# P1's stores on ScalarE's queue, two kept blocks in u's buffer, four operands no longer kept

## The chip, the core and the metric

The kernel runs on one core of a Trainium2 chip. The metric is the time of one execution on the device in microseconds; the time of a kernel is the median of several runs. A core has TensorE (matmuls into PSUM), VectorE, ScalarE, GpSimd and SyncE. In the profile they are PE (its weight loads apart, as PEld), DVE, ACT, POOL and SP. DMAs are issued by SyncE, ScalarE and GpSimd, each in the order of its own instructions.

## The reference, cut to what matters

```python
def reference(x, router_logits, expert_weights):
    # x (16, 512, 512), router_logits (16, 512, 8), expert_weights (8, 512, 2048), float32
    probs = softmax(router_logits, axis=-1)
    for e in range(8):
        output += probs[:, :, e:e+1] * np.matmul(x, expert_weights[e])
    return output          # (16, 512, 2048) float32
```

The sum over experts is one matrix product: the left side has 8192 rows (tokens) and 8 x 512 columns, x times the probability of expert e side by side; the right side is the eight weight matrices on top of each other, 4096 x 2048.

## The kernel before, in words

**Two levels of fast multiplication.** The large product is cut in two by two: token blocks of 256 rows go in pairs a = 2q and b = 2q + 1 (q = 0 to 15), the experts in two groups of four, the output columns in two halves of 1024. Instead of eight products of such parts the kernel does seven, called P1 to P7, with sums of left parts, of right parts and of results around them. Each of them is again done in seven steps (1, 5, 6, 2, 7, 3, 4 in that order, `STEPS`, line 389) of eight matmuls of 128 x 512, and in some stages four of the steps are done with a third level (`Third`, line 674). TensorE accumulates in PSUM; the other engines make the operands and carry the results on.

**Stages.** A stage holds two products (14 steps, "slots" of about 1.73 us), rarely one. In order: P1 of q = 2 to 15 is stages 0 to 6 (of q = 0, 1 it is done at the very start in another way); P2 is 7 to 14; P5 of q = 0, 1 is stage 15 (`k5`); P6 of q = 0 alone is stage 16; P6 of q with P5 of q + 1 is 17 to 30; P6 of 15 with P7 of 14 is 31 (`k7`); P4 and P7 are 32 to 46; 47 (`k3`) has the last P4 and P3 of q = 0; 48 has P3 of q = 14 and 15; 49 to 54 have P3 of 1 to 12 in pairs; 55 has P3 of 13. Stages 0 to 6, 8 to 12 and 49 to 54 have the third level.

**Order of work.** All engines keep the order in which the program writes their instructions. `at(stage, slot, ...)` (line 751) hangs work on a slot. VectorE's operands are tasks in one queue: `later(cost, make)` (line 415) appends one with a cost in us; `slack()` (line 420) runs at each slot, moves a counted clock on by 1.73 and writes down tasks until VectorE's counted clock has caught up; `evacuated()` counts 0.61 for a sum of a result. `need` (line 410) writes down what is needed at once. Loads of x and p blocks for a stage begin two stages before (`start_loads`, line 846), in nine buffers of `xpool`; P1's x blocks 16 to 30 are cast by GpSimd into the one buffer called u (`x_room`, line 435) and transposed by SyncE's DMA (line 463).

**What the change touches.**
- P1's results of q go to DRAM (`kept`) by `sink` in `product` (line 804): four blocks (0,0), (0,1), (1,0), (1,1) of 128 x 512, all stored from GpSimd's queue by `pool`. Step 2 gives (0,0) and step 4 gives (1,0), both copied from PSUM by ScalarE (line 627); step 7 gives (1,1) and step 3 (0,1), by VectorE (line 630).
- `Base.fetch` (line 738) loads such a block back from SyncE's queue into one of 13 buffers h. `fetch_at` (line 951) hangs the fetches of P2 on slots of the stage before it (lines 960 to 965), those of P6 on lines 993 to 997. P6 first takes P5's block off it (`joined`, line 989). The block is then the tile in which the result is summed and from which it is stored.
- `KEEP` (line 762): for these q the left operand of P6 is stored from SyncE's queue (line 1289, `kept_left`) and in P3 it is loaded back from ScalarE's queue (line 1290, `Operand`, line 563), so that P3's left operand is one product of x and p, less the loaded one. For other q the loaded part is made anew (`second` in `Left.makes`, line 507): x and p of the second block are loaded and multiplied into u, and then taken off.
- The odd block of the weights, (0, 1): `cast_odd` (line 1076) casts its matrices 12, 11, 22 and 21 in two halves each at the slots of line 1116; `odd_t` (line 1081) makes three differences and sums of them, each one VectorE instruction of 128 x 4096; `odd_t4` (line 1097), at stage 15, slot 4, takes the last off matrix 21.

Of the kernel before, what the change touches and what calls it, by code (L numbers as in the profile page):

```python
# [31 lines left out]
def kernel(  # L32
# [17 lines left out]
    C = H // P  # L50
    HE = E // 2
    NB = 512
# [12 lines left out]
    zpool = ctx.enter_context(tc.tile_pool(name="zpool", bufs=8))  # L65
# [8 lines left out]
    def h_tile(shape, dtype):  # L74
        return hpool.tile(shape, dtype, name="h", tag="h")

    def half():
        return h_tile([P, NB], f32)

    lg0 = [cpool.tile([P, 4, E], f32, name=f"lg0_{t}") for t in range(2)]  # L80
    for q, begin in enumerate((nc.scalar, nc.sync)):
        rows = ds(2 * q * HQ, HQ)
        begin.dma_start(out=lg0[0][:, ds(2 * q, 2), :],
                        in_=router_logits.flatten_outer_dims()[rows].rearrange("(p j) e -> p j e", p=P))
# [15 lines left out]
    def note(i):  # L100
        last[i.ins.engine] = i.ins
        if ordered[0]:
            tc.keep_in_program_order(i)

    def dve(i):
        last[i.ins.engine] = i.ins
        tc.keep_in_program_order(i)
# [3 lines left out]
    def tt(o, a, b, op):  # L111
        dve(nc.vector.tensor_tensor(out=o, in0=a, in1=b, op=op))  # L112
# [9 lines left out]
    def sp(o, i):  # L122
        note(nc.sync.dma_start(out=o, in_=i))

    def pool(o, i, **how):
        note(nc.gpsimd.dma_start(out=o, in_=i, **how))  # L126

    def bank():
        return psum.tile([P, NB], f32, name="ps", tag="ps")
# [29 lines left out]
    def kept_w(what, kn):  # L159
        if (what, kn) not in stored:  # L160
            stored[what, kn] = dram.tile([C, P, 2, NB] if what in TWOS else [P, K8, NB], f16, name="wd")
        kept_t = stored[what, kn]
        return kept_t.rearrange("a p b n -> p a b n") if what in TWOS else kept_t
# [47 lines left out]
    def cast_x(j):  # L211
        pool(xs0[:, ds(j, 2), :], x_f[ds(j * HQ, HQ), :].rearrange("(j p) h -> p j h", p=P))
# [350 lines left out]
    class Operand:  # L563
# [86 lines left out]
    class Split:  # L650
# [74 lines left out]
    def out_rows(q, odd, cols, tn):  # L725
        t, n = tn
        return out_f[ds((2 * q + odd) * HQ + t * HP, HP), ds(cols * NH + n * NB, NB)]

    def to_out(q, odd, cols, **how):
        return lambda tn, o: pool(out_rows(q, odd, cols, tn), o, **how)  # L730

    class Base:
# [2 lines left out]
        def __init__(self, source):  # L735
            self.source, self.t = source, {}

        def fetch(self, tn):
            self.t[tn] = half()
            sp(self.t[tn], self.source(tn))  # L740

        def __call__(self, tn):
# [8 lines left out]
    def at(stage, slot, make):  # L751
        hooks.setdefault((stage, slot), []).append(make)

    def add(*products):
        stages.append(products)
        return len(stages) - 1
# [2 lines left out]
    right = {r: Right() for r in (2, 5, 6, 7, 4, 3)}  # L759
    right[1] = Right(w, {p: Task(2.2, sums[p]) for p in (6, 7, 4)})  # L760
    lefts, xs, ps_, bases = {}, {}, {}, {}
    KEEP = range(1, 14)

    def xblock(h):
        if h not in xs:
            xs[h] = XBlock(h)
        return xs[h]

    def left_of(r, q, fresh=True):
# [15 lines left out]
        if r == 6:  # L785
            pt = PBlock(a, P1)
            return Left(xblock(a), pt, of=lefts[5, q]), [xblock(a), pt]
        if r == 3 and q in KEEP:
            pt = PBlock(a, P2)
# [7 lines left out]
    def kept_rows(q):  # L797
        return lambda tn: kept[q][tn[1], ds(tn[0] * HP, HP), :]

    def product(r, q, **how):  # L800
        left, loads = left_of(r, q)
        lefts[r, q] = left
        p = None
        if r == 1:
            def sink(tn, o):
                pool(kept_rows(q)(tn), o)
            p = Product(right[1], left, sink)
        elif r == 2:
            if q >= 14:
                base = products[1, q].o.__getitem__  # L810
            else:
                base = bases[2, q] = Base(kept_rows(q))
            p = Product(right[2], left, to_out(q, 0, 0), base)
        elif r == 5:
            bases[6, q] = m1 = Base(kept_rows(q))
            m1.task = {}

            p = Product(right[5], left, to_out(q, 1, 0))
        elif r == 6:
            m1 = bases[6, q]  # L820

            def base(tn):
                need(m1.task[tn])
                return m1.t[tn]
            p = Product(right[6], left, to_out(q, 0, 1), base)
            if q in KEEP:
                left.kept = dram.tile([P, 2, K8, HQ], f16, name=f"kept_left_{q}")
        elif r == 7:
            if q < 14:
                base = bases[7, q] = Base(lambda tn: out_rows(q, 0, 1, tn))  # L830
            else:
                base = products[6, q].o.__getitem__
            p = Product(right[7], left, to_out(q, 1, 1), base)
        elif r == 4:
            p = Product(right[4], left, to_out(q, 1, 0, accum_op=ADD), products[7, q].o.__getitem__)
        else:
            p = Product(right[3], left, to_out(q, 0, 1, accum_op=ADD), **how)
        p.loads = loads
        products[r, q] = p
        return p  # L840
# [107 lines left out]
        for n in range(end, len(slots)):  # L948
            held.append(lambda n=n: one(n))

    def fetch_at(stage, slot, base, *tns):
        for tn in tns:
            at(stage, slot, lambda tn=tn: base.fetch(tn))


    for q in range(2, 16, 2):
# [1 line left out]
    forget(*range(0, 28, 2))  # L958
    rest = [14, 15] + list(range(14))
    for i in range(0, 16, 2):  # L960
        k = add(product(2, rest[i]), product(2, rest[i + 1]))
        for slot, tn in zip((8, 10, 12, 13), INNER):
            for q in rest[i:i + 2]:
                if q < 14:
                    fetch_at(k if tn == (1, 0) else k - 1, 3 if tn == (1, 0) else slot, bases[2, q], tn)
    xs.clear()
    k5 = add(product(5, 0), product(5, 1))
    add(product(6, 0))
# [20 lines left out]
    def joined(q, tn):  # L989
        m1 = bases[6, q]  # L990
        m1.task[tn] = later(0.61, lambda: tt(m1.t[tn], m1.t[tn], products[5, q].o[tn], SUB), True)

    for q in range(16):
        k = k5 + 1 + q
        duo = len(stages[k - 1]) == 2
        for slot, tn in zip((2, 4, 6, 8) if duo else (1, 2, 3, 4), INNER):
            fetch_at(k - 1, slot, bases[6, q], tn)
        for tn, where in zip(INNER, ((k - 1, 12), (k - 1, 13), (k - 1, 13), (k, 3)) if duo
                             else ((k - 1, 5), (k - 1, 6), (k - 1, 6), (k, 3))):
            at(*where, lambda q=q, tn=tn: joined(q, tn))  # L1000
        if q < 14:
            for slot, tn in zip((7, 9, 11, 17), INNER):
                fetch_at(k7 + q + 1 + slot // 14, slot % 14, bases[7, q], tn)
# [37 lines left out]
    b21, t1, t2, t3 = {}, {}, {}, {}  # L1041
# [29 lines left out]
    ODD = 0, 1  # L1071


    made = {}

    def cast_odd(q, e):
        if e == 0:
            made[q] = new_w()
        cast_w(q, ODD, e, made[q][:, ds(e * C, C), :])

    def odd_t():

        def make1():
            t1[ODD] = made[11]
            tt(t1[ODD], made[11], made[12], SUB)

        def make3():
            tt(made[12], made[22], made[12], SUB)
            pool(kept_w("t3", ODD), made.pop(12))

        def make2():
            t2[ODD] = made[22]
            tt(t2[ODD], made[22], t1[ODD], ADD)
        for make in (make1, make3, make2):
            later(2.2, make)

    def odd_t4():
        def make():
# [14 lines left out]
        return one(4, b[1, 0], b[1, 0], b[1, 1]) if all_ else sixth  # L1113

    last2 = k5 - 1
    for stage, slot, q, e in ((9, 9, 12, 0), (9, 13, 12, 1), (10, 4, 11, 0), (10, 9, 11, 1), (11, 2, 22, 0), (11, 7, 22, 1), (14, 8, 21, 0), (14, 12, 21, 1)):
        at(stage, slot, lambda q=q, e=e: cast_odd(q, e))
    at(12,5, odd_t)
    for i, kn in enumerate(((0, 0), (1, 1), (1, 0))):
# [130 lines left out]
    ends = []  # L1250
    HALVES = "2a", "2b"

    def act_dma(o, i):
        note(nc.scalar.dma_start(out=o, in_=i))

    def step_at_end(p, step=finish.step):
        if p not in HALVES:
            return step(p)
# [27 lines left out]

    for q in KEEP:
        for k, slot in enumerate((1, 5)):
# [61 lines left out]
```

## Time and profile before

| | us |
|---|---|
| median of 3 runs | 1366.07 |
| lowest, highest of them | 1363.82, 1367.02 |
| the profiled execution | 1371.11 |
| its span, first to last instruction | 1369.4 |
| TensorE busy in the span | 1358.2 (99%) |
| VectorE busy | 1154.2 (84%) |
| GpSimd busy | 415.7 (30%) |
| ScalarE busy | 204.5 (15%) |
| HBM read, written | 218.92 MB, 167.97 MB |

A row of a list in order of time has start and length in us, the engine (a q behind it is its DMA issuing), the line, the operation, output <- input by the program's names, the shapes and how many instructions it merges; in brackets stands how long the engine was idle before it, and what ended that. A row of groups has the busy time in us, the mean of one in ns, and the idle time before them. A row of waits has the total in us, how often, and the longest. A row of DMA issues has the count, the size, and the median us from issue to landing. Line 112 is the helper of all VectorE's sums and products, line 132 of all matmuls, line 126 of GpSimd's DMAs, line 123 of SyncE's.

### The profile page before, as it was taken

How to read it: one execution, taken by the hardware profiler on the slowest of the kernel's cores; microseconds unless marked ns; L12 is line 12 of the kernel's file. 1: busy time of each engine (PE TensorE's matmuls, PEld its weight loads, DVE VectorE, ACT ScalarE, POOL GpSimd, SP SyncE). 2: the span in 40 equal slices, each digit the busy share in tenths (PEclk: the TensorE clock that was granted, in tenths of full speed). 3: DMA queues.
4: the chain of work that ended last, by engine and by line, in shares of the span. 5: the costliest groups of instructions: out<-in, count | busy, mean ns of one | idle time of the engine just before them, and what ended most of it. 6: DMA issues, size and time to landing. Idle time of an engine off the chain costs nothing.

```text
span 1369.4 us, 18641 instructions
## 1 busy us (share of the span) xinstructions
PE 1358.2 (99%) x6825; PEld 666.0 (49%) x6825; DVE 1154.2 (84%) x1429; ACT 204.5 (15%) x390; POOL 415.7 (30%) x650
## 2 busy tenths in 40 slices
PE   9999999999999999999999999999999999999998
PEld 4555555555444444444444444444444444456564
DVE  7987489988999888888878988888889797898873
ACT  3332221111011111111111100000000000123221
POOL 3133332231213243343323222232332422233232
PEclk9999999999999999999999999999999999999999
DMA  9999998999898999999999988889898979999896
GB/s 194 220 268 225 279 218 260 275 301 358 262 326 269 276 298 301 316 290 321 281 297 313 397 301 223 211 239 209 229 251 227 246 200 292 294 226 240 198 212 109
DMA packets 198811, 357.74 MB, mean 261 GB/s; under 512 B 53312, under 2 KB 90432, under 8 KB 194368
## 3 DMA queue, kind: packets, MB, share of 16 engines
q0 software_dynamic: 90448, 183.02, 56.5%
q1 hardware_dynamic: 100208, 133.56, 33.1%
q10 hardware_dynamic: 8064, 39.99, 7.9%
q8 instruction: 53, 0.87, 0.2%
q14 instruction: 38, 0.31, 0.1%
HBM read 218.92 MB, written 167.97 MB: 283 GB/s over the span
## 4 chain that ended last, share of the span: by engine, by line
PE 88%; issue 4%; DMA 3%; DVE 3%; POOL 1%; SPq 0%; POOLq 0%; ACT 0%; DVEq 0%
PE ps L132 88%; DMA out_dram<-h 2%; POOL out_dram L126 1%; DVE z L112 1%; DMA xT<-u 1%; DMA w<-in_expert_weights_dram 1%; DMA pT<-p_dram 1%; DVE h L112 0%; DVE t L112 0%; DVE u L112 0%; DVE s L112 0%; DVE d L112 0%; POOL wd L126 0%; DVE w L112 0%; POOL w L126 0%
## 5 line engine op out<-in xcount | busy, mean ns | idle before, releaser
L132 PE MATMUL ps<-w,z 128*128 128x512 f16 x5128 | 1094.5, 373 | 0.3 <-DMA w<-in_expert_weights_dram 0.3
L132 PEld LDWEIGHTS <-z 128*128 128x128 f16 x5272 | 516.1, 98 | 578.4 <-issue 5.1
L126 POOL DMA_DIRECT2D out_dram<-h x380 | 249.3, 662 | 710.2 <-ACT h L638 344.4
L112 DVE TENSOR_TENSOR h<-ps,h 128x512 f32<-128x512 f32 x415 | 283.4, 687 | 127.5 <-PE ps L132 114.5
L112 DVE TENSOR_TENSOR z<-xT,pT 128x2048 f16<-128x2048 f16 x216 | 261.5, 1218 | 23.8 <-DMA kept_left<-z 7.7
L132 PE MATMUL ps<-w,d 128*128 128x512 f16 x880 | 201.4, 382 | 2.2 <-DVE ps L112 2.2
L132 PEld LDWEIGHTS <-d 128*128 128x128 f16 x880 | 86.6, 98 | 103.8 <-issue 5.1
L112 DVE TENSOR_TENSOR z<-z,d 128x2048 f16<-128x2048 f16 x110 | 132.2, 1217 | 0.0
L112 DVE TENSOR_TENSOR w<-w 128x1024 f16<-128x1024 f16 (+2 forms) x100 | 108.1, 1091 | 13.6 <-DMA w<-in_expert_weights_dram 8.6
L638 ACT COPY h<-ps 128x512 f32<-128x512 f32 x64 | 37.5, 586 | 509.4 <-PE ps L132 461.6
L627 ACT COPY h<-ps 128x512 f32<-128x512 f32 x90 | 52.8, 587 | 273.8 <-PE ps L132 244.5
L112 DVE TENSOR_TENSOR d<-z 128x1024 f16<-128x1024 f16 x110 | 74.1, 687 | 1.5
L126 POOL DMA_DIRECT2D w<-in_expert_weights_dram x77 | 57.1, 753 | 44.4 <-DMA wd<-w 31.0
L624 ACT COPY h<-ps 128x512 f32<-128x512 f32 x90 | 51.6, 590 | 121.7 <-PE ps L132 97.5
L126 POOL DMA_DIRECT2D wd<-w x90 | 53.1, 605 | 43.9 <-DVE w L112 29.1
L126 POOL DMA_DIRECT2D kept<-h x56 | 30.9, 552 | 114.0 <-ACT h L627 85.0
L132 PEld LDWEIGHTS <-s 128*128 128x128 f16 x576 | 56.4, 98 | 10.6 <-issue 0.4
L132 PE MATMUL ps<-t,s 128*128 128x256 f16 x432 | 58.9, 273 | 0.1
L112 DVE TENSOR_TENSOR ps<-ps,d 128x256 f32<-128x256 f32 x72 | 30.2, 430 | 25.6 <-PE ps L132 25.5
L112 DVE TENSOR_TENSOR ps<-ps,h 128x512 f32<-128x512 f32 (+1 forms) x66 | 45.3, 688 | 4.7 <-PE ps L132 4.7
L112 DVE TENSOR_TENSOR h<-h 128x512 f32<-128x512 f32 (+2 forms) x69 | 45.1, 676 | 3.6 <-DMA out_dram<-h 3.5
L112 DVE TENSOR_TENSOR u<-xT,pT 128x2048 f16<-128x2048 f16 x38 | 46.3, 1218 | 0.0
(61 smaller groups left out, 354.8 us busy)
## 6 DMA issues: line engine op xcount, KB each, us to landing
out_dram<-h POOLq DMA_DIRECT2D x380, 256.0 KB, 7.3
pT<-p_dram SPq DMA_DIRECT2D x125, 256.0 KB, 7.0
h<-kept SPq DMA_DIRECT2D x120, 256.0 KB, 8.4
w<-wd ACTq DMA_DIRECT2D x25, 1024.0 KB, 10.6
xT<-x SPq DMA_DIRECT2D x77, 256.0 KB, 7.5
wd<-w POOLq DMA_DIRECT2D x76, 256.0 KB, 6.3
w<-in_expert_weights_dram POOLq DMA_DIRECT2D x35, 512.0 KB, 11.4
h<-out_dram SPq DMA_DIRECT2D x60, 256.0 KB, 5.4
```

What stands on the lines that cost most here:

```text
L112: dve(nc.vector.tensor_tensor(out=o, in0=a, in1=b, op=op))
L126: note(nc.gpsimd.dma_start(out=o, in_=i, **how))
L132: note(nc.tensor.matmul(ps, z, w, start=start, stop=stop, skip_group_check=True))
L624: act(nc.scalar.copy(o[tn], q if p == 5 else x))
L627: act(nc.scalar.copy(o[TN[p]], b if p == 2 else x))
L638: act(nc.scalar.copy(o[tn], b))
```

## The change

P1's blocks (0,0) and (1,0) are stored from ScalarE's queue, behind ScalarE's own copies. The casts of matrix 21 of the odd block move from slots 8 and 12 of stage 14 to slots 3 and 8, and each task of `odd_t` becomes two halves. In three of P2's stages (8, 10 and 12) the blocks (0,0) of both products, and for odd q up to 13 the blocks (0,0) and (1,1) of P6, are loaded into the two halves of u's buffer instead of two buffers h. `KEEP` loses q = 2, 4, 6 and 8.

```diff
+    def act_dma(o, i):
+        note(nc.scalar.dma_start(out=o, in_=i))
...
-        def fetch(self, tn):
-            self.t[tn] = half()
+        def fetch(self, tn, pair=None):
+            if pair is None:
+                self.t[tn] = half()
+            else:
+                if not pair:
+                    two = zpool.tile([P, 2, NB], f32, name="r", tag="u", bufs=1)
+                    pair += [two[:, i] for i in range(2)]
+                self.t[tn] = pair.pop()
             sp(self.t[tn], self.source(tn))
...
-    KEEP = range(1, 14)
+    KEEP = (1,3,5,7,9,10,11,12,13)
...
             def sink(tn, o):
-                pool(kept_rows(q)(tn), o)
+                (act_dma if tn[1] == 0 else pool)(kept_rows(q)(tn), o)
...
     for i in range(0, 16, 2):
+        pair = [] if i // 2 in (1,3,5) else None
         k = add(product(2, rest[i]), product(2, rest[i + 1]))
         for slot, tn in zip((8, 10, 12, 13), INNER):
             for q in rest[i:i + 2]:
                 if q < 14:
-                    fetch_at(k if tn == (1, 0) else k - 1, 3 if tn == (1, 0) else slot, bases[2, q], tn)
+                    fetch_at(k if tn == (1, 0) else k - 1, 3 if tn == (1, 0) else slot, bases[2, q], tn,
+                             pair=pair if tn == (0, 0) else None)
...
         duo = len(stages[k - 1]) == 2
+        pair = [] if q in range(1, 14, 2) else None
         for slot, tn in zip((2, 4, 6, 8) if duo else (1, 2, 3, 4), INNER):
-            fetch_at(k - 1, slot, bases[6, q], tn)
+            fetch_at(k - 1, slot, bases[6, q], tn, pair=pair if tn in ((0, 0), (1, 1)) else None)
...
     def odd_t():
+        halves = [ds(e * C, C) for e in range(2)]
-        def make1():
+        def make1(h):
             t1[ODD] = made[11]
-            tt(t1[ODD], made[11], made[12], SUB)
+            tt(t1[ODD][:, h], made[11][:, h], made[12][:, h], SUB)
...
         for make in (make1, make3, make2):
-            later(2.2, make)
+            for h in halves:
+                later(1.14, lambda make=make, h=h: make(h))
...
-    for stage, slot, q, e in ((9, 9, 12, 0), (9, 13, 12, 1), (10, 4, 11, 0), (10, 9, 11, 1), (11, 2, 22, 0), (11, 7, 22, 1), (14, 8, 21, 0), (14, 12, 21, 1)):
+    for stage, slot, q, e in ((9,9,12,0),(9,13,12,1),(10,4,11,0),(10,9,11,1),(11,2,22,0),(11,7,22,1),(14,3,21,0),(14,8,21,1)):
```

More of the change, by code (lines that the diff above doesn't have):

```diff
@@ L949, in run, with fetch_at @@
             held.append(lambda n=n: one(n))
-    def fetch_at(stage, slot, base, *tns):
+    def fetch_at(stage, slot, base, *tns, pair=None):
         for tn in tns:
-            at(stage, slot, lambda tn=tn: base.fetch(tn))
+            at(stage, slot, lambda tn=tn: base.fetch(tn, pair))
     for q in range(2, 16, 2):
@@ L1081, in odd_t, with make3, make2 @@
     def odd_t():
-        def make1():
+        halves = [ds(e * C, C) for e in range(2)]
+        def make1(h):
             t1[ODD] = made[11]
-            tt(t1[ODD], made[11], made[12], SUB)
[L1087 to L1091, printed above, removed]
+            tt(t1[ODD][:, h], made[11][:, h], made[12][:, h], SUB)
+        def make3(h):
+            tt(made[12][:, h], made[22][:, h], made[12][:, h], SUB)
+            if h is halves[1]:
+                pool(kept_w("t3", ODD), made.pop(12))
+        def make2(h):
             t2[ODD] = made[22]
-            tt(t2[ODD], made[22], t1[ODD], ADD)
+            tt(t2[ODD][:, h], made[22][:, h], t1[ODD][:, h], ADD)
         for make in (make1, make3, make2):
-            later(2.2, make)
+            for h in halves:
+                later(1.14, lambda make=make, h=h: make(h))
     def odd_t4():
@@ L1251 @@
     HALVES = "2a", "2b"
-    def act_dma(o, i):
-        note(nc.scalar.dma_start(out=o, in_=i))
     def step_at_end(p, step=finish.step):
```

## The prediction

> **What bounds the kernel now.** I read the page first, then the list of waits on TensorE, then TensorE's instructions in order of time, then the busy times by stretch. The page gives the span, and the waits view says for what TensorE stood still after its first ten microseconds.
>
> ```profile
> span 1369.4 us, 18641 instructions
> PE ps L132 <- DVE ps L112: 5.3, 2, 3.1
> ```
>
> TensorE waits twice, both times for VectorE. Outside these places it repeats the same intervals to a hundredth, so it is the bound, and a change can only win what these two places lose. The stretches below run from one repeating matmul group to its next; the columns are the stretch and its length, the busy time of TensorE, its weight loads, VectorE, ScalarE and GpSimd, the granted clock, the share of the DMA engines and GB/s.
>
> ```profile
> 131.10:154.48 23.38, 23.38 (x139) 13.32 (x136) 15.55 (x22) 6.95 (x14) 9.39 (x15) 1.00 1.13 266
> 154.48:182.79 28.31, 25.22 (x138) 13.76 (x136) 14.99 (x21) 6.95 (x14) 6.60 (x11) 0.94 0.97 242
> ...
> 381.34:405.51 24.17, 24.17 (x113) 10.94 (x112) 22.06 (x21) 2.90 (x5) 6.15 (x11) 1.00 1.06 325
> 393.42:405.51 12.09, 12.09 (x57) 5.49 (x56) 10.80 (x11) 1.73 (x3) 4.06 (x8) 1.00 1.10 317
> 405.51:445.80 40.29, 38.11 (x169) 16.89 (x168) 36.13 (x40) 5.26 (x9) 11.64 (x20) 0.96 0.90 270
> ...
> 1209.43:1233.12 23.69, 23.59 (x138) 13.29 (x136) 22.85 (x30) 6.95 (x14) 9.22 (x11) 1.00 0.89 236
> 1233.12:1256.50 23.38, 23.38 (x138) 13.30 (x136) 19.70 (x25) 6.95 (x14) 7.18 (x9) 1.00 0.94 219
> ```
>
> The first place, in P1's stage 5, costs 28.31 - 23.38 = 4.93 us. The second, between P5's stage 15 and P6's single stage 16, costs 40.29 - 24.17 - 12.09 = 4.03 us. A third, at the start of P3, costs 23.69 - 23.38 = 0.31 us. Each of the first two is an idle gap and then a stretch at a lower clock: 3.09 us idle and 28.31 x (1 - 0.94) = 1.7 us in the first. For the second, the instruction and its window are
>
> ```profile
> 428.58 2.64 PE L132 MATMUL ps<-w,d 128*128 128x512 f16 x8 [2.18 <-DVE ps L112]
> 428.50:434.00 5.50, 5.42 (x18) 0.69 0.91 253
> ```
>
> that is 2.18 us idle and 5.50 x (1 - 0.69) = 1.71 us of lost clock. The profiled execution took 1371.11 us, 1.71 us more than its span. Without the three places it would be 1371.11 - 4.93 - 4.03 - 0.31 = 1361.84 us. The median shown, 1366.07, is 4.23 us above that, the profiled execution 9.27 us. So a usual run carries about 4.23 / 9.27 = 0.46 of these losses, and I scale what is left of them by that.
>
> The Trainium skill, page "TensorE: Matmul & The Clock Gate", section "HAM oscillation — how this bites in real kernels", asks only for no idle gap above about 3.4 us. This trace disagrees: 2.18 us was enough for a slower stretch. By the page a gap of 1 us costs itself alone.
>
> **Edit 1, P1's (0,0) and (1,0) stores on ScalarE's queue.** GpSimd's queue around stages 3 and 4, SyncE's transposes, VectorE's instructions and TensorE's stall behind them:
>
> ```profile
> 125.38 0.77 POOL L126 DMA_DIRECT2D w<-in_expert_weights_dram  x1
> 128.08 0.55 POOL L126 DMA_DIRECT2D kept<-h  x1 [1.93 <-DVE w L112]
> 128.62 0.72 POOL L126 DMA_DIRECT2D wd<-w  x1
> 129.33 0.56 POOL L126 DMA_DIRECT2D kept<-h  x1
> 131.09 0.72 POOL L126 DMA_DIRECT2D wd<-w  x1 [1.20 <-DVE w L112]
> 131.81 0.56 POOL L126 DMA_DIRECT2D kept<-h  x1
> 136.04 0.76 POOL L126 DMA_DIRECT2D w<-in_expert_weights_dram  x1 [3.67 <-DMA kept<-h]
> 137.41 0.54 POOL L126 DMA_DIRECT2D kept<-h  x1 [0.60 <-DMA kept<-h]
> 141.33 1.53 POOL L126 DMA_DIRECT2D u<-in_x_dram  x2 [3.38 <-DMA w<-in_expert_weights_dram]
> ...
> 151.39 10.03 SPq L463 DMA_TRANSPOSE xT<-u  x4
> ...
> 164.37 1.23 DVE L112 TENSOR_TENSOR z<-xT,pT 128x2048 f16<-128x2048 f16 x1 [4.40 <-DMA xT<-u]
> 165.51 0.76 DVE L112 TENSOR_TENSOR ps<-ps,d 128x256 f32<-128x256 f32 x2
> 165.99 1.18 PE L132 MATMUL ps<-t,z 128*128 128x256 f16 x8 [3.09 <-DVE ps L112]
> ```
>
> Count eight issues on from the cast at 125.38: the eighth is the load of u at 141.33, and it waits for that cast to land. The cast at 136.04 likewise waits for a store eight places earlier. GpSimd's queue thus runs with eight transfers outstanding, and it is late: by the program the load of x blocks 28 and 30 stands at the start of stage 4 (about 132), behind the cast at 136.04. Hence the transposes at 151.39, the product at 164.37, and behind it on VectorE the PSUM sum at 165.51 on which TensorE stands. Half of P1's 56 stores leave this queue, about two of every four `kept` rows here, so the eighth before the u load is a transfer of some 8 us earlier. I expect the load 5 to 9 us sooner; 4.40 us are enough to clear the wait. Gain 4.93 us in the profiled execution; 0 if the load does not move.
>
> ScalarE issues 28 DMAs for it. The nearest rows are its own store at the end and a group of three loads:
>
> ```profile
> 1365.82 0.34 ACTq L1254 DMA_DIRECT2D out_dram<-h  x1
> 371.13 16.12 ACTq L180 DMA_DIRECT2D w<-wd  x3
> ```
>
> At 0.34 us each this is 9.5 us over seven stages in which ScalarE is busy 6.95 of 23.38 us: nothing, hidden by its idle time; without that cover it is those 9.5 us. The second row bounds it from above: three issues of ScalarE took 16.12 us, so they can be held too. Behind a held store ScalarE's PSUM copies would wait, and TensorE for them. If SyncE and ScalarE share a limit of eight as GpSimd has one, the order of a P1 stage (two p loads, two stores, two x stores, a store, four transposes, a store) puts an earlier store, or a transpose of half a stage before, in the eighth place ahead of a ScalarE store. I take 0.
>
> The Trainium skill, page "DMA: Bandwidth & Descriptors", section "Issuing engines are not separate DMA queues", speaks against this edit: the transfers run on the same 16 engines whoever starts them, and only the issuing time is saved. By it the u load would land no sooner and the 4.93 us would stay; this is the first rival below.
>
> **Edit 2, the odd block's last casts sooner, its sums in halves.** The cast of matrix 21 is issued in two halves, and VectorE waits for the later one:
>
> ```profile
> 389.86 0.77 POOL L126 DMA_DIRECT2D w<-in_expert_weights_dram  x1
> 397.70 0.77 POOL L126 DMA_DIRECT2D w<-in_expert_weights_dram  x1
> ...
> 398.13 2.29 DVE L112 TENSOR_TENSOR w<-w 128x4096 f16<-128x4096 f16 x1 [1.26 <-DMA w<-wd]
> 410.62 6.82 DVE L112 TENSOR_TENSOR w<-w 128x4096 f16<-128x4096 f16 x3 [1.21 <-DMA w<-in_expert_weights_dram]
> ```
>
> From 410.62 to 428.5 VectorE has no gap, so its 1.21 us of waiting is what TensorE loses later. With the casts at slots 3 and 8 the second goes out where the first does now, about 8 us sooner, and the wait is gone. (The first moves ahead of two result stores on GpSimd's queue that wait for ScalarE; it takes the weight buffer that P2 lets go first, and the `w<-wd` loads take those let go two and four slots later, before their turn on ScalarE's queue.) So 2.18 - 1.21 = 0.97 us of gap stays. Whether a gap of 0.97 us costs the slow stretch no row shows; 0.31 us did not, 2.18 did, and it is nearer to the former. Gain 1.21 + 1.71 = 2.92 us; from -1 (the earlier cast delays the `w<-wd` load behind the 1.26 us) to 4.03. The sums of `odd_t` become six instructions for three of the same total; they run in stage 13, where no TensorE wait exists: 0.
>
> **Edit 3, two kept blocks in u's place.** Same loads, same sums, another buffer. TensorE's two waits above are all that its view has; none lies from 434 to 1209, where these loads are, and that unbroken work of TensorE hides them: 0. u is free there from the transposes of P1 until P7. A pair's buffer is asked for again two stages later; if its stores are late, SyncE's next loads stand behind it, and the loss is below that of one gap in each place, up to 4.03 us, which I give no weight.
>
> **Edit 4, four operands not kept.** P6 drops eight stores from SyncE's queue in the same stretch without a wait: 0. P3 drops four loads from ScalarE's queue and adds, for q = 2, 4, 6 and 8, two x and p loads and two products by VectorE each. VectorE at the turn to P3:
>
> ```profile
> 1176.88 0.69 DVE L112 TENSOR_TENSOR h<-ps,h 128x512 f32<-128x512 f32 x1 [2.41 <-DMA out_dram<-h]
> 1213.45 2.35 DVE L112 TENSOR_TENSOR z<-z,d 128x2048 f16<-128x2048 f16 x2
> 1215.72 0.76 DVE L112 TENSOR_TENSOR ps<-ps,d 128x256 f32<-128x256 f32 x2
> ...
> L112 DVE TENSOR_TENSOR u<-xT,pT 128x2048 f16<-128x2048 f16 x38 | 46.3, 1218 | 0.0
> ```
>
> Eight products by 1.218 us are 9.7 us, 2.4 us per stage. Stages like 1233 to 1256 have 23.38 - 19.70 = 3.68 us of idle VectorE and hide that. The turn does not: VectorE is full from 1176.88, and TensorE already loses 0.31 us to the sum at 1215.72. Counting the queue by its rule (lines 415 to 428, with the costs that the code names), two of the new products come ahead of that sum, and one of the two `z<-z,d` falls behind it: net one instruction of (1215.72 - 1213.45) / 2 = 1.14 us. I take +1.14 us; from 0 (if the 2.41 us wait at 1176.88 shrinks) to 2.4 + 1.71.
>
> **The sum.** 1371.11 - 4.93 - 2.92 + 1.14 = 1364.40 us for an execution like the profiled one. 1364.40 - 1361.84 = 2.56 us of losses are left; a usual run carries 0.46 of them, 1.2 us: **1363.0 us**, 0.22% below the median of before.
>
> **Rivals.**
> - P1's stall stays, because the sixteen engines and not the queue make the load late (their share is 1.13 in the row from 131.10). For it: that share. Against: the exact eighth-place waits. 1364.40 + 4.93 = 1369.33, scaled 1361.84 + 0.46 x 7.49 = 1365.3 us.
> - The second stall stays, since another late load (the 1.26 us) takes the cast's place: 1364.40 + 2.92 = 1367.32, scaled 1364.4 us.
> - Slower: P3's x and p buffers. Nine of them are enough for two and a half stages of four loads, not for six per stage; then the loads of the subtracted factor start when VectorE lets go of the stage before, and by the queue's rule some 15 us remain until it needs them.
>
> ```profile
> pT<-p_dram SPq DMA_DIRECT2D x125, 256.0 KB, 7.0
> ```
>
>  Such a load lands in 7.0 us at the median, which speaks against. From about 15 us on VectorE waits, its 1.3 us of spare time per stage is gone, and each of the stages 50 to 52 gives a gap of 1 us and a slow stretch of 1.71: 1363.0 + 3 x 2.71 = 1371.1 us.
> - Slower: ScalarE's stores are held like its loads at 371, a few us in each of P1's seven stages: 1363 + 7 x 2 = 1377 us.
>
> **How the numbers follow.** About 0.2% tells this kernel from no change: below 1363.3 or above 1368.8. The forecast has 0.50 (own range 1361.8 to 1363.8; a tenth of it within 0.2%), P1's stall stays 0.14, the second stays 0.14, P3's buffers 0.17, held stores 0.05. Faster 0.46, same 0.32, slower 0.22. The range goes from 1361.5, no loss left, to 1368.5, part of the way to P3's rival.
>
> **What would show it.** Right: the load of u issued near 133, no gap near 163; VectorE without a wait for the cast near 409 and a gap of about 1 us or none near 427; a gap of about 1.2 us near 1208 and none later in P3; ScalarE's P1 stores at 0.3 to 0.4 us each with no wait ahead. Wrong: the load of u still near 141; ScalarE standing before a store; TensorE waiting for `sum` or `u` products in stages 50 to 53.

## The result, and the profile after

| | before | changed |
|---|---|---|
| median of 4 runs each, us | 1365.54 | 1374.93 |
| lowest to highest, us | 1363.82 to 1367.02 | 1373.64 to 1376.95 |
| the profiled execution, us | 1371.11 | 1375.57 |
| its span, us | 1369.4 | 1373.9 |

The ratio is 1.0071, with a 95% interval of 1.0052 to 1.0089: the changed kernel is 9.4 us slower. One execution of a later run, e12, took 6337.15 us and is left out of its ratio. The prediction had 1363.0 us and a range that ended at 1368.5. All line numbers behind line 126 are higher by 3 in the changed kernel: matmuls are line 135, ScalarE's copies of step 1 line 623.

The list of waits on TensorE has a new first line. Its columns are the total in us, how often, the longest.

```profile
PE ps L135 <- ACT ps L623: 7.8, 2, 4.7
...
PE ps L135 <- DVE ps L112: 1.2, 1, 1.2
```

VectorE was the one waited for in before; now ScalarE is, for the copy of step 1's sum to a second PSUM bank (the order is TensorE's step 1, ScalarE's copy, TensorE's step 2 on top of the copy). TensorE in order of time has these at the places the prediction named, and at two new ones:

```profile
73.18 5.30 PE L135 MATMUL ps<-w,d 128*128 128x512 f16 x16 [3.15 <-ACT ps L623]
149.87 6.24 PE L135 MATMUL ps<-w,d 128*128 128x512 f16 x16 [4.67 <-ACT ps L623]
...
433.67 1.89 PE L135 MATMUL ps<-w,d 128*128 128x512 f16 x8
...
1220.99 1.03 PE L135 MATMUL ps<-t,s 128*128 128x256 f16 x8 [1.18 <-DVE ps L112]
```

The row at 433.67 is the one that stood 2.18 us in before, now without a wait. The row at 1220.99 is the turn to P3, 1.18 us. The old wait near 163 is gone, but P1 has two waits in its place, each with a stretch of slow clock behind it. Columns of the stretches as in the prediction:

```profile
73.18:76.60 3.42, 3.42 (x9) 1.29 (x9) 3.32 (x6) 1.43 (x3) 0.00 (x0) 0.52 1.22 216
149.87:155.20 5.33, 5.33 (x13) 1.93 (x13) 1.72 (x2) 2.01 (x4) 0.00 (x0) 0.50 1.18 247
```

The first costs 3.15 + 3.42 x (1 - 0.52) = 4.8 us, the second 4.67 + 5.33 x (1 - 0.50) = 7.3 us: 12.1 us in all. Less these and the 1.34 us that TensorE is late at the turn to P3, the profiled execution is 1375.57 - 12.1 - 1.34 = 1362.1 us, as against the 1361.84 us of before without its losses. So the loss is in P1, and ScalarE's order of work at the end of stage 3 and in stage 4 shows where it comes from:

```profile
127.00 0.59 ACT L630 COPY h<-ps 128x512 f32<-128x512 f32 x1 [1.14 <-PE ps L135]
127.62 0.33 ACTq L129 DMA_DIRECT2D kept<-h  x1
128.73 0.58 ACT L630 COPY h<-ps 128x512 f32<-128x512 f32 x1 [1.14 <-PE ps L135]
138.03 0.33 ACTq L129 DMA_DIRECT2D kept<-h  x1
138.40 0.36 ACT L715 COPY ps<-ps 128x256 f32<-128x256 f32 x1 [9.09 <-DMA xT<-u]
...
142.61 0.58 ACT L630 COPY h<-ps 128x512 f32<-128x512 f32 x1 [2.51 <-PE ps L135]
148.82 0.33 ACTq L129 DMA_DIRECT2D kept<-h  x1
149.25 1.06 ACT L623 COPY ps<-ps 128x512 f32<-128x512 f32 x2 [6.05 <-DMA x<-xT]
```

A store (ACTq) should go out right behind its copy, as the one at 127.62 does. The one at 138.03 goes out 8.72 us after its copy's end (128.73 + 0.58 = 129.31), the one at 148.82 goes 5.63 us after its own (143.19). The copies behind a held store wait with it, and the profile puts these waits down to SyncE's transfers, a transpose of u and a store of x, with which the stored block has nothing to do. Their times to landing, in the list of DMA issues (the last column, us), for the transpose issued at 123.97 and the store of x issued at 141.08:

```profile
xT<-u SPq DMA_TRANSPOSE x1, 14.0
...
x<-xT SPq DMA_DIRECT2D x1, 256.0 KB, 7.7
```

123.97 + 14.0 = 138.0, and the store at 138.03 goes out; 141.08 + 7.7 = 148.8, and the one at 148.82 does. The trace names the completion counter of each DMA. SyncE and ScalarE together use eight of them in turn, and GpSimd eight of its own; an issue waits until the transfer before it on the same counter has landed. For the stores held over 2 us in P1 of the changed kernel, worked out from the trace:

| store issued | its copy ended | the transfer before it on its counter | that one landed |
|---|---|---|---|
| 57.56 | 55.21 | SyncE's x store, issued 52.86 | 57.48 |
| 72.13 | 68.03 | SyncE's p load, issued 64.47 | 72.06 |
| 109.13 | 105.93 | SyncE's transpose, issued 99.71 | 109.05 |
| 138.03 | 129.31 | SyncE's transpose, issued 123.97 | 137.96 |
| 148.82 | 143.19 | SyncE's x store, issued 141.08 | 148.75 |
| 215.66 | 205.21 | SyncE's transpose, issued 212.04 | 215.58 |
| 222.60 | 216.63 | SyncE's p load, issued 216.05 | 222.52 |

Each goes out 0.07 or 0.08 us after that landing. The x store issued at 141.08 was late itself: it went out 0.06 us after the transpose of u issued at 125.94 had landed, at 141.02. Only the stores at 72.13 and 148.82 stand just ahead of a copy on which TensorE waits; the others are held in time that ScalarE has to spare. The waits of ScalarE from 40 to 230 us say the same by groups. In before none of them is for a transfer:

```profile
ACT ps L712 <- PE ps L132: 49.9, 13, 7.2
ACT h L627 <- PE ps L132: 48.6, 28, 8.0
...
ACT ps L620 <- DVE ps L112: 3.6, 5, 0.7
```

In the changed kernel six lines are, 36.9 us in all, of which these are four:

```profile
ACT h L630 <- DMA xT<-xs: 10.8, 1, 10.8
ACT ps L715 <- DMA xT<-u: 9.1, 1, 9.1
ACT h L630 <- DMA pT<-p_dram: 8.5, 2, 6.3
ACT ps L623 <- DMA x<-xT: 6.0, 1, 6.0
```

The load of u, which edit 1 was to bring forward, and VectorE's casts around 404, which edit 2 was to free, read so now (GpSimd and VectorE in order of time):

```profile
141.59 0.71 POOL L126 DMA_DIRECT2D u<-in_x_dram  x1 [4.36 <-DMA xT<-u]
```

```profile
404.52 2.29 DVE L112 TENSOR_TENSOR w<-w 128x4096 f16<-128x4096 f16 x1 [1.15 <-DMA w<-wd]
...
415.72 6.81 DVE L112 TENSOR_TENSOR w<-w 128x4096 f16<-128x4096 f16 x3
```

The load of u goes out at 141.59 where before had 141.33, not near 133. GpSimd's queue was free for 4.36 us, and the load waited for a transpose: u is one buffer, and the transposes of the stage before still read it. That TensorE's wait near 163 is gone all the same is not the load's doing: the four transposes of u behind it landed 3.7 to 6.0 us after their issue, where before had 9.1 to 15.6 us, and TensorE came there some 12 us later. The wait for the cast of matrix 21 is gone, the wait for `w<-wd` is as before.

### The profile page after: what moved, and what is told of

Same layout as the page of the kernel before. It is cut to its first block, busy times and chain, and to the rows that moved or that the text cites. A ratio compares the mean times of both kernels' runs of the same rounds, so it can differ in the third digit from the quotient of the medians.

```text
span 1373.9 us, 18619 instructions
## 1 busy us (share of the span) xinstructions
PE 1359.0 (99%) x6825; PEld 665.8 (48%) x6825; DVE 1163.5 (85%) x1440; ACT 204.0 (15%) x390; POOL 399.8 (29%) x622
## 4 chain that ended last, share of the span: by engine, by line
PE 86%; issue 4%; DMA 4%; DVE 3%; POOL 1%; ACT 0%; SPq 0%; ACTq 0%; POOLq 0%; DVEq 0%
PE ps L135 86%; DMA out_dram<-h 2%; DVE z L112 1%; DMA xT<-u 1%; POOL out_dram L126 1%; DMA x<-xT 1%; DVE h L112 1%; DMA pT<-p_dram 1%; DMA w<-in_x_dram 0%; DVE u L112 0%; DVE s L112 0%; DVE d L112 0%; POOL wd L126 0%; SPq L466 0%; DVE ps L112 0%
## 5 line engine op out<-in xcount | busy, mean ns | idle before, releaser
L126 POOL DMA_DIRECT2D out_dram<-h x360 | 237.8, 664 | 638.5 <-ACT h L641 284.6
L112 DVE TENSOR_TENSOR h<-ps,h 128x512 f32<-128x512 f32 x401 | 274.6, 687 | 132.3 <-PE ps L135 115.0
L641 ACT COPY h<-ps 128x512 f32<-128x512 f32 x51 | 29.9, 586 | 450.7 <-PE ps L135 448.4
L630 ACT COPY h<-ps 128x512 f32<-128x512 f32 x90 | 52.7, 586 | 284.8 <-PE ps L135 262.9
L627 ACT COPY h<-ps 128x512 f32<-128x512 f32 x90 | 51.6, 590 | 120.8 <-PE ps L135 109.3
L126 POOL DMA_DIRECT2D kept<-h x28 | 15.6, 558 | 140.3 <-DVE h L112 140.0
L112 DVE TENSOR_TENSOR u<-xT,pT 128x2048 f16<-128x2048 f16 x46 | 56.0, 1217 | 0.0
L112 DVE TENSOR_TENSOR z<-z,u 128x2048 f16<-128x2048 f16 x42 | 51.2, 1218 | 0.3
L112 DVE TENSOR_TENSOR ps<-ps,h 128x512 f32<-128x512 f32 (+1 forms) x53 | 36.3, 686 | 4.5 <-PE ps L135 4.2
```

The costliest lines, as they stand in the source:

```text
L627: act(nc.scalar.copy(o[tn], q if p == 5 else x))
L630: act(nc.scalar.copy(o[TN[p]], b if p == 2 else x))
L641: act(nc.scalar.copy(o[tn], b))
```

## The experiments

Each chip's runs have their own runs of the kernel before beside them. A ratio is to those; in brackets its 95% interval. It is worked out over the executions and can differ a little from the quotient of the two medians (by up to 0.0007 here).

| run | what is in it | median, us | before, us | ratio |
|---|---|---|---|---|
| e1 | edits 2, 3, 4 | 1362.53 | 1363.81 | 0.9987 [0.9973, 1.0000] |
| e2 | edit 1 | 1370.67 | 1363.81 | 1.0047 [1.0027, 1.0066] |
| e3 | edit 2 | 1362.72 | 1363.81 | 0.9985 [0.9970, 1.0001] |
| e4 | edit 4 | 1363.99 | 1363.81 | 0.9998 [0.9984, 1.0013] |
| e5 | edit 3 | 1365.83 | 1365.43 | 1.0001 [0.9984, 1.0018] |
| e6 | edits 2, 3 | 1367.76 | 1365.43 | 1.0012 [0.9997, 1.0027] |
| e7 | changed, only (0,0) on ScalarE | 1372.33 | 1365.43 | 1.0053 [1.0036, 1.0070] |
| e8 | changed, (1,0) stored later | 1371.69 | 1365.43 | 1.0040 [1.0024, 1.0055] |
| e9 | changed, the stores on SyncE | 1370.24 | 1365.35 | 1.0032 [1.0016, 1.0048] |
| e10 | edits 3, 4 | 1362.59 | 1365.35 | 0.9985 [0.9973, 0.9998] |
| e11 | P2's half of edit 3 | 1362.25 | 1365.35 | 0.9971 [0.9962, 0.9980] |
| e12 | edits 2, 3, 4 again | 1363.10 | 1365.35 | 0.9984 [0.9974, 0.9993] |
| e13 | changed again | 1373.33 | 1365.02 | 1.0063 [1.0045, 1.0081] |
| e14 | edit 1 again | 1374.49 | 1365.02 | 1.0073 [1.0047, 1.0098] |
| e15 | before again | 1364.84 | 1365.02 | 0.9992 [0.9972, 1.0012] |

### Which edit loses: e1 to e4

e1 takes the ScalarE stores out of the changed kernel, e2 puts them alone into before:

```diff
-                (act_dma if tn[1] == 0 else pool)(kept_rows(q)(tn), o)
+                pool(kept_rows(q)(tn), o)
```

> The changed kernel with edit 1 alone undone: all of P1's stores are back on GpSimd's queue. Theory A (the loss is ScalarE, which stands at P1's stores, with its PSUM copies behind it): TensorE's two waits for ScalarE's copies near 73 and 150 us (4.78 + 7.31 = 12.09 us with their slow stretches in the changed kernel) are gone; what is left is 1361.84 + 1.57 us at the turn to P3 and up to 4.93 us of the old stall near 163, so 1363 to 1368 us, 7 to 12 us below the changed kernel. Theory B (the loss comes from the four operands not kept, or from the pairs in u's buffer): the time stays near 1374, within 2 us of the changed kernel.

> The kernel before with edit 1 alone: P1's (0,0) and (1,0) stores on ScalarE's queue. Theory A: P1 runs as in the changed kernel, TensorE waits for ScalarE's copies near 73 and 150 us for 12.1 us with their slow stretches, the old stall near 163 is gone, the stall near 428 (3.8 us) is still there: 1374 to 1379 us. Theory B: 1361 to 1366 us, the old stall in P1 gone and nothing in its place.

e1 lies at 1362.53 us, 0.5 us below the range of theory A, since the old stall near 163 is not there either. No wait of TensorE in P1 at all is left in its profile, and theory B is out. After the first ten microseconds its TensorE waits for this alone:

```profile
PE ps L135 <- DVE ps L112: 0.8, 1, 0.8
PE ps L135 <- DMA w<-in_expert_weights_dram: 0.4, 1, 0.4
```

e2 is 0.47% slower than before. Its TensorE, in order of time:

```profile
72.74 3.61 PE L135 MATMUL ps<-w,d 128*128 128x512 f16 x16 [2.75 <-ACT ps L623]
145.16 5.30 PE L135 MATMUL ps<-w,d 128*128 128x512 f16 x16 [2.12 <-ACT ps L623]
429.38 1.89 PE L135 MATMUL ps<-w,d 128*128 128x512 f16 x8 [1.30 <-DVE ps L112]
```

Same places, same releaser; the waits are shorter than in the profiled execution of the changed kernel, and the time was below the 1374 to 1379 us expected (e13 and e14 come back to that).

e3 has edit 2 alone, as in the diff of the change, and e4 has `KEEP` alone.

> The kernel before with edit 2 alone: the last casts of the odd block sooner and its sums in halves. My theory: the stall near 428 (3.8 us in the profile of before) is gone whole as in the changed kernel, P1's stall near 163 stays as it is: 1 to 4 us below before, 1362 to 1365 us. Rival: the stall near 428 was removed in the changed kernel only because P1 ran later or because of the pairs in u's buffer; then it stays here and the time is that of before.

By the trace the rival held in e3, though the median, 1362.72 us, lies in the range of my theory; the interval of the ratio reaches 1.0001, so a gain is not shown. The old stall near 163, which was to stay, is not there. VectorE no longer waits for the cast, but longer for the load in front of it, and TensorE stands about as long as in another kernel on this chip that casts as before does (e4: 1.83 us). VectorE's row, then TensorE's:

```profile
394.19 2.29 DVE L112 TENSOR_TENSOR w<-w 128x4096 f16<-128x4096 f16 x1 [3.04 <-DMA w<-wd]
```

```profile
423.33 1.89 PE L132 MATMUL ps<-w,d 128*128 128x512 f16 x8 [2.12 <-DVE ps L112]
```

That load is one of ScalarE's. It was issued at 380.81, when SyncE's p load before it on its counter, issued at 368.36, had landed at 380.74. So the same turn that holds the stores in P1 holds this load.

> The kernel before with edit 4 alone: P6's operands 2, 4, 6 and 8 are not kept for P3. My theory: the wait at the turn to P3 grows from 0.27 us to 1.3 us and nothing else changes: 1.0 to 1.2 us above before. Rival B (P3's stages are overloaded by six loads and one more product per subtracted factor): waits of 1 us and more in the stages behind the turn, 5 to 9 us above before.

TensorE was 1.29 us late at the turn to P3 in e4's profile and nowhere behind it: my theory's place and size. In the medians 1 us does not show (1363.99 beside 1363.81, the interval goes from 0.9984 to 1.0013). Rival B is out.

### Edit 3, and what pays for what: e5, e6, e10

> The kernel before with edit 3 alone: P2's and P6's pairs of kept blocks in u's buffer. The prediction priced this edit at 0: a time within 1 us of before and TensorE's wait near 423 as long as with edit 4 alone (2.0 us). New theory, from edit 2 alone (wait still 2.3 us, VectorE 3.0 us behind ScalarE's w<-wd load issued at 380.8) beside the changed kernel without edit 1 (no wait, that load issued at 376.7): the pairs let GpSimd's cast of xs and SyncE's loads behind it go 2 to 4 us sooner, and with them ScalarE's w<-wd load. Then here VectorE's wait for w<-wd is below 1 us and TensorE's wait near 423 is 0 to 1.3 us.

> The kernel before with edits 2 and 3, without the ScalarE stores and with all operands kept. New theory: edit 2 takes the wait for the cast away and edit 3 the wait for w<-wd, so TensorE's wait near 423 is gone whole, and the turn to P3 costs 0.3 us instead of 1.0 to 1.3: 1361 to 1362 us where before has 1363.8, 1 us below the changed kernel without edit 1. If edit 3 has no part in it: a wait of 2 us near 423 as with edit 2 alone, and 1362.7 us.

In both, TensorE has no wait near 423: the new theory. VectorE does not wait for `w<-wd` in e5, and 0.82 us in e6. GpSimd's cast of xs goes out at 347.66 and 346.59 (e3: 349.49). But the times do not fall: e6 has 1367.76 us where 1361 to 1362 us were expected, since new waits come in P6. e6's TensorE, and SyncE's longest wait of its kind in e5 from 560 to 690 us:

```profile
583.78 5.30 PE L132 MATMUL ps<-w,d 128*128 128x512 f16 x16 [2.32 <-DVE ps L112]
674.16 6.19 PE L132 MATMUL ps<-w,z 128*128 128x512 f16 x27 [1.89 <-DVE h L112]
```

```profile
SPq L123 <- DMA out_dram<-r: 28.9, 3, 13.9
```

A pair's buffer is asked for again before its results have been stored from it. SyncE stands up to 13.9 us for that, with VectorE's loads behind it. VectorE waits 11.0 us there for `h<-kept` loads in e5. With what follows them TensorE's waits cost 2.9 us in e5 and 6.7 us in e6, counted from matmul to matmul against e11. e1 differs from e6 by edit 4 alone and has 0.2 us there. But its SyncE stands for the pair's stores as long:

```profile
SPq L123 <- DMA out_dram<-r: 29.5, 3, 16.6
```

So that stand alone is not the loss. What differs is what VectorE waits for in that stretch: `h<-kept` and `kept_left<-z`, the stores of operands that edit 4 thins out, together hold it 19.4 us in e5 and 18.9 us in e6, but 7.4 us in e1 and 1.2 us in e10.

> The kernel before with edits 3 and 4, without edit 2 and without the ScalarE stores. From edit 3 alone (no wait near 423, new waits of 2.9 us in P6 between 580 and 625 while SyncE stands up to 13.9 us for the pair's stores) and from the changed kernel without edit 1 (no wait in P6 over 0.2 us): edit 4 pays for edit 3, and edit 2 pays for nothing. Expected: no wait near 423, at most 0.5 us in P6, 1.0 to 1.3 us at the turn to P3, the time of the changed kernel without edit 1 within 1 us. If edit 2 matters: 2 us or more near 423.

e10 is as expected: no wait near 423, none in P6, 1.34 us at the turn to P3, and 0.9985 of before, the same as e1 and e12 with edit 2. So edit 4 pays for P6's pairs, and edit 2 adds nothing that can be measured to edits 3 and 4.

### What holds ScalarE: e7, e8, e9

```diff
-                (act_dma if tn[1] == 0 else pool)(kept_rows(q)(tn), o)
+                (act_dma if tn == (0, 0) else pool)(kept_rows(q)(tn), o)
```

> The changed kernel with only the (0,0) stores on ScalarE's queue (14 instead of 28 there); (1,0) is back on GpSimd's. Theory A (place in ScalarE's order): the (0,0) stores have 6 us of idle ScalarE behind them, the (1,0) stores stand just ahead of step 1's PSUM copies; so here TensorE never waits for a ScalarE copy, and the time is that of the changed kernel without edit 1, 1362 to 1364 us. Theory C (each store on ScalarE costs its share, or its transfers slow SyncE's transposes): about half of the loss stays, 1366 to 1368 us.

e8 keeps all 28 and moves the (1,0) stores behind the copies:

```diff
             def sink(tn, o):
+                if tn == (1, 0):
+                    deferred.append(lambda: act_dma(kept_rows(q)(tn), o))
+                else:
...
                 product.post(p)
+        store_deferred()
         after(stage, 4)
```

> The changed kernel with the same 28 stores on ScalarE's queue, but each (1,0) store is issued behind the PSUM copies of steps 1 and 5 of the next stage instead of ahead of them. Theory A: no store stands ahead of step 1's copies any more; TensorE's waits for them (12.1 us with their slow stretches in the changed kernel) are gone, a store held over 3 us may still delay a later copy by 1 to 2 us: 1362 to 1367 us. Theory C (number of stores or their transfers): as the changed kernel, 5 to 9 us above before.

Both came out slower than theory A had it, and I drop the part of it that was about the place. The waits for step 1's copies are gone in both, but the hold went to other copies. e7's ScalarE, and then TensorE in e7:

```profile
145.94 0.33 ACTq L129 DMA_DIRECT2D kept<-h  x1
147.05 0.59 ACT L630 COPY h<-ps 128x512 f32<-128x512 f32 x1 [1.14 <-PE ps L135]
160.97 0.34 ACTq L129 DMA_DIRECT2D kept<-h  x1
161.36 0.36 ACT L715 COPY ps<-ps 128x256 f32<-128x256 f32 x1 [13.72 <-DMA xT<-u]
```

```profile
161.77 1.87 PE L135 MATMUL ps<-w,z 128*128 128x256 f16 x8 [4.38 <-ACT ps L715]
```

With 14 stores instead of 28 ScalarE was held 13.3 us at one of them, longer than at any in the changed kernel: the transpose before it on its counter, issued at 149.88, landed at 160.90. Six microseconds of spare time were no cover for that. e8's waits are 2.62 us for line 715 at 136.89 and 1.53 us for line 627 at 200.01, each behind a store held for a transpose. By its time alone e8 is also what theory C had (5 to 9 us above before: it is 6.3). But the number of stores is not what counts, as half of them lost 6.9 us in e7, above theory C's 1366 to 1368 us; in both traces the held stores wait for their turn. Whether the stores' own transfers also slow SyncE's transposes, the other part of theory C, no run separates.

```diff
-                (act_dma if tn[1] == 0 else pool)(kept_rows(q)(tn), o)
+                (sp if tn[1] == 0 else pool)(kept_rows(q)(tn), o)
```

> The changed kernel with the same 28 stores on SyncE's queue instead of ScalarE's. Theory A, as the two runs before left it (a store of ScalarE takes its turn behind SyncE's last eight transfers, whatever place it has in ScalarE's order, and the copies behind it wait): now SyncE does the waiting, ScalarE's copies have nothing ahead of them, and TensorE waits for no ScalarE copy in P1: 1361 to 1366 us; what may be late instead are SyncE's transposes, in which case TensorE waits for VectorE near 160. Theory C (28 stores away from GpSimd's queue are the loss, whoever issues them): 4 to 9 us above before.

ScalarE has no wait for any transfer from 40 to 230 us in e9, as theory A said, so it was the store instructions in its queue that stopped it. The time, 1370.24 us, is outside the 1361 to 1366 us. It is 4.9 us above before, which is in theory C's range too, so the time does not decide; the trace does. SyncE now stood 70.9 us for ScalarE's copies, and VectorE waited 5.41 us for a transpose, which the expectation named as the other case. e9's GpSimd and TensorE:

```profile
143.63 0.71 POOL L126 DMA_DIRECT2D u<-in_x_dram  x1 [11.27 <-DMA xT<-u]
```

```profile
166.88 1.86 PE L135 MATMUL ps<-t,z 128*128 128x256 f16 x8 [4.10 <-DVE ps L112]
```

GpSimd had been idle for 11.27 us and still could not issue the load of u, because the transposes were reading u. A free GpSimd queue is not what that load lacked here.

### A faster version, and the size of edit 1: e11 to e15

e11 puts edit 3 alone into before and takes P6's half of it out again:

```diff
-        pair = [] if q in range(1, 14, 2) else None
+        pair = None
```

> The kernel before with P2's half of edit 3 alone: the pairs in u's buffer in three stages of P2, none in P6, all operands kept. Theory: P2's pairs are what bring the loads of stage 14 forward, so the wait near 423 is gone or below 0.5 us; without pairs in P6 no new wait there, without edit 4 only 0.3 us at the turn to P3: TensorE loses under 1 us in all, 1 to 2 us below the changed kernel without edit 1 and below before. Rival: the P6 pairs are needed for it, then the wait of 2 us near 423 is here as in before.

> The changed kernel with edit 1 alone undone, a second time, on the same chip as the run with P2's pairs alone: whether it beats before. From its first run (0.9987 of before): 1 to 3 us below before, and 1 us above the run with P2's pairs alone, the cost of the turn to P3.

e11, with P2's pairs and nothing else, is the fastest by its median: 0.9971 of before (3.1 us between the medians), and its 11 runs lie between 1361.30 and 1362.67 us, while before's on that chip reach 1369.91. e12 has edits 2 to 4 a second time and gives 0.9984, 0.85 us above e11 in the medians; the intervals of e10, e11 and e12 overlap. The list of waits on e11's TensorE has 0.6 us for VectorE in all:

```profile
PE ps L132 <- DVE h L112: 0.4, 2, 0.2
PE ps L132 <- DVE ps L112: 0.2, 1, 0.2
```

> The changed kernel itself, on the same chip as edit 1 alone. If edit 1's cost is the same in both and the two earlier results differ by the chips they ran on, this is within 2 us of edit 1 alone, plus 1.1 us at the turn to P3 and less the wait near 423 (1.5 to 2 us), both 6 to 9 us above before; TensorE's waits for ScalarE's copies in P1 sum to the same in both profiles within 2 us. If edits 2 to 4 make edit 1 dearer: 3 us or more above edit 1 alone.

> Edit 1 alone, a second time, beside the changed kernel on one chip: 6 to 9 us above before, as in its first run or by the chip; TensorE's waits for ScalarE's copies in P1 as in the changed kernel within 2 us.

On one chip the changed kernel and edit 1 alone agree: 1.0063 and 1.0073 of before, with intervals that overlap. Their TensorE waits 4.2 and 6.0 us for ScalarE's copies in P1, within the 2 us expected; e14 is 9.5 us above before, a little over the 6 to 9 us. So edits 2 to 4 do not make edit 1 dearer; e2's smaller loss came on another chip, and its interval overlaps e14's.

> The kernel before, to see whether its profiled execution was a usual one. Four profiles of kernels with the same P1 had no wait near 163. If the 4.93 us there were the mark of a long execution: no wait near 163 here, and 2 to 4 us near 428. If it is usual: 3 us or more near 163.

Before has no wait near 163 in this profile; its loss is in one place, with a slow stretch behind it (TensorE in order of time):

```profile
424.98 3.38 PE L132 MATMUL ps<-w,d 128*128 128x512 f16 x8 [3.41 <-DVE ps L112]
```

## Why the prediction was wrong, point by point

**Edit 1, ScalarE's cost: "I take 0".** This is the step that failed. The prediction saw that SyncE and ScalarE might share a limit of eight, and counted that "an earlier store, or a transpose of half a stage before" would stand in the eighth place. The limit was right, the order only in part, and it took the wait for harmless. Three of the seven stores that were held over 2 us stood behind a transpose, and half a stage, some 12 us, is no cover for that: the eight transposes of u that before issues from 117 to 156 landed 9.1 to 15.6 us after their issue. The two stores that TensorE paid for stood behind a p load and an x store, issued only 3.6 and 2.1 us before the stored blocks were ready. The row that bounded the cost from above, three issues of ScalarE that took 16.12 us, was the same mechanism: the second of them went out at 385.64, when the first, the transfer before it on its counter, had landed at 385.56. The rival "ScalarE's stores are held like its loads at 371", 1377 us, is what happened (1374.93); it had 0.05. That its number came so near is in part luck: it had 2 us in each of seven stages, and TensorE lost 4.8 and 7.3 us in two places. Two of the signs that the prediction had named for being wrong came, the load of u still near 141 and ScalarE standing before a store. Measured, the step costs 12.1 us in the profiled execution, and by e1 and the first result 1.0071 / 0.9987, some 0.8% or 11 us, in the medians.

**Edit 1, the gain: "5 to 9 us sooner", 4.93 us.** Wrong twice. The load of u does not only stand in GpSimd's queue, it also needs the one buffer u: in before, the last transpose that reads it was issued at 123.22 and landed at 137.3, so 4 us sooner than 141.33 was the most to be had. In the changed kernel it was 0.3 us later, in e9 it waited for the transposes with GpSimd idle; with the stores where before has them, e1, e3 to e6, e10, e11 and e15 issue it between 135.2 and 138.5. And the 4.93 us were not a loss of usual executions: the five profiles with P1 as in before, e3, e4, e5, e6 and e15, have no such wait, and neither have e10 and e11. Scaling the whole profile's losses by 0.46 could not see that one of them was rare. The rule that the prediction quoted against this edit (the Trainium skill, page "DMA: Bandwidth & Descriptors", section "Issuing engines are not separate DMA queues") is borne out so far: the first load of u landed at 153.63, in before at 151.38. But that rule names no cost of another issuing engine either, and these runs show 11 us.

**Edit 2, 2.92 us.** In the changed kernel the wait near 428 is gone whole, more than the 2.92 us. But edit 2 is not the reason: alone it leaves 2.12 us (e3), because another late load, `w<-wd`, takes the cast's place. That was the prediction's second rival, with the load named. Edit 3 alone removes the wait (e5): the five profiles with P2's pairs and P1's stores as in before (e1, e5, e6, e10, e11) have none, and the four without the pairs (before, e3, e4, e15) have 1.8 to 3.4 us. With edit 1 alone the wait was 1.30 us in e2 and none in e14, so it can also go without either edit where P1 runs late; why is open.

**Edit 3, 0.** Wrong, and both ways. P2's half brings GpSimd's casts and with them the loads of stage 14 forward (the cast of xs goes out at 347.90 and the `w<-wd` load at 378.88 in e11, at 350.32 and 382.13 in e15), and e11, which has it alone, has the whole gain. Why the pairs let that cast go sooner was not followed. P6's half costs 2.9 to 6.7 us without edit 4 (e5, e6). The prediction saw SyncE's wait for the pair's stores and gave it no weight; with edit 4 that wait is as long and costs nothing (e1, e10).

**Edit 4, +1.14 us at the turn to P3.** Right: TensorE's lateness there grew from 0.27 us in before to 1.34 us in the changed kernel and e10 and to 1.29 us in e4. The queue's order, counted through, gave place and size: two new products stand ahead of the sum, at 1204.93 and 1216.51, and one `z<-z,d` behind it, at 1221.18. Rival 3, P3's buffers, did not come. That edit 4 takes stores from SyncE in P6 was priced at 0; beside edits 2 and 3 it is worth 6.5 us in the profiles (6.7 us in e6, 0.2 in e1) and some 3.4 us by the ratios (1.0012 and 0.9987).

**A gap of 1 us costs itself alone.** Borne out at the turn to P3: after the 1.18 us the granted clock is 1.00.

```profile
1220.99:1226.00 5.01, 5.01 (x35) 3.41 (x35) 4.98 (x7) 2.55 (x5) 0.60 (x1) 1.00 1.10 261
```

## What to carry to other kernels

A DMA that is moved to a compute engine's queue brings along the wait for its turn: find in the trace which engines share the completion counters, take the transfer that many places ahead, and compare its time to landing with the time until that engine's next work on the path. A buffer's last reader limits a load as much as its queue does; check both before a gain is booked. One profile's stall may be rare: a second profile of the kernel before (e15) had no trace of the largest gain that was booked, and running the edits alone showed that a small part of the change gives, as far as the intervals tell, all that is gained without edit 1.

## What the runs showed of the hardware that was not expected

Between 2.1 and 3.4 us the length of TensorE's gap does not tell whether a slow stretch follows. After 2.12 us at 145.16 the clock was 0.68 (e2), after 2.12 us at 423.33 it was 1.00 (e3), and after 3.35 us at 73.60 it was 1.00 (e14). Of the gaps looked at in these traces none up to 1.89 us (e6, at 674.16) had a slow stretch behind it, and all from 3.41 us on (e15, at 424.98, clock 0.70) had one. The stretches behind the three gaps, one line of each kernel:

```profile
145.16:150.50 5.34, 5.34 (x17) 2.09 (x17) 3.92 (x5) 2.02 (x5) 0.00 (x0) 0.68 1.19 249
```

```profile
423.33:429.00 5.67, 5.67 (x27) 2.60 (x27) 4.90 (x7) 0.59 (x1) 0.56 (x1) 1.00 0.97 214
```

```profile
73.60:78.00 4.40, 4.40 (x21) 2.04 (x21) 4.33 (x7) 2.60 (x5) 0.00 (x0) 1.00 1.20 207
```

Nor is the time of a transpose fixed: those of u in P1 landed after 2.7 to 16.6 us in these traces. The held stores differ from profile to profile too: the one at 148.82 was held 5.63 us, its like in e13, at 145.32, only 2.23 us. That the spread of the landings decides this is likely, but no run shows it by itself.
